# A hybrid decoder layer on one core: small loads moved to lanes and other queues, unread products and ordered low parts at two seams

## The chip, the cores and the metric

One core of a Trainium2 chip runs the kernel. The metric is the time of the core in microseconds; the figure for a kernel is the median of its runs. All times here are in us unless marked ns.

## The reference

The reference is one decoder layer on a row block `x` of 256 tokens by 2048 channels, in fp32. Three sub-layers follow one another, each of the form x = x + rmsnorm(f(rmsnorm(x) * gain)) * gain:

```
mixer:  one projection w_in, whose columns go to three head groups
        A  dilated window attention, with a bias looked up in rel_bias_table
        B  causal gating by 128x128 triangular matrices
        C  RWKV-7 time mixing, with decays sigmoid(tanh(h w_lo) w_up + w0)
        then the output projection w_out
cross:  attention of 4 heads over 256 memory tokens (their norm has the gain mem_src_gain)
FFN:    w_up, a causal depthwise convolution of width 3 (taps ffn_conv_w, ffn_conv_b), gelu gate, w_down
```

## The kernel before

**Products.** Weights and activations are fp32. Each 512 KB block of weights is loaded raw (`raw`, four buffers, SP's queue), and `split()` makes two halves from it: ScalarE casts it to a high part `hi` (line 234), VectorE subtracts this from the raw block for the low part `lo` (line 236). TensorE then makes three products for each pair of blocks, high by high, activation low by weight high and activation high by weight low, on lines 266, 268 and 271 in the mixer's projection, 287 in the FFN's first projection and 324, 326 and 330 in the projections that put weights on the moving side. The activation halves `h` come from a transposition of `x` on TensorE (line 389), ScalarE for the high part times the norm's gain (line 375) and VectorE for the low part (line 376). The gains for that are rows in `grow`, turned to columns `gpar` by one transposition on line 469.

**Stages.** The mixer's projection runs to about 300 us, w_out and the cross attention to about 605 us, and the FFN from there to the end. The seam between the last two is the chain of line 1328 (squares of the cross attention's output), line 1340 (the residual sum, `row`), line 389 (transposition), lines 375 and 376 (`h`), line 287 (first FFN product).

**Order.** Each engine takes its instructions in a fixed order that a scheduler writes from priorities, from pins (`issue_after`) and from lanes. A lane is a Python generator whose `yield` gives the planner an amount of TensorE time; the planner lets the projections' products run and puts a lane's next step behind them. The lanes of the mixer are one chain of `decays`, three `keys` and `inverse`, one of `values`, and three `state`.

**What stands in the first 100 us.** The start loads `x` (8 blocks) and the first weight block on SP's queue, `grow` on ScalarE's queue in two parts, and later on SP's queue, between weight blocks, the rows of the small parameters (`prow`), the bias table with its one-hot matrix (`tab`, `oneh`, `lnc`) and the convolution's taps (`crow`). The bias table's product stands on line 531, the taps' transpositions on line 543. `decays` multiplies the tanh block `zl` by three blocks `wa` (line 642), which share one buffer and are loaded on ScalarE's queue (lines 633 and 634), takes sigmoids (line 647) and then exponentials (lines 662 and 663). ScalarE loads a table whenever it changes between the two. GpSimd fills `BN`, `BR` and `ze` (lines 557, 558 and 591) and loads `lg` (line 616).

Of the kernel before, what the change touches and what calls it, by code (L numbers as in the profile page):

```python
# [12 lines left out]
F32 = mybir.dt.float32  # L13
# [159 lines left out]
def hybrid_block(tc, a, out, dbg=None):  # L173
    nc = tc.nc
    dbg = dbg or {}
    with ExitStack() as ctx:
# [50 lines left out]

        def split(rv, nk, nco):
            hi = mk(wp, "hi", 3, (P, 1024), F32R)
# [3 lines left out]
            with tc.high_priority(offset=AHEAD):  # L233
                nc.scalar.copy(hv, rv)  # L234
                with tc.issue_after(gcopy.ins):
                    nc.vector.tensor_tensor(lv, rv, hv.bitcast(F32), op=ALU.subtract)  # L236
# [182 lines left out]

        def over_rows(r):  # L420
# [31 lines left out]
        grow = sp.tile([4 * KT, P], F32, name="grow")  # L452
        with tc.high_priority(offset=4 * AHEAD):
            nc.scalar.dma_start(grow[:3 * KT, :], gains[0:6:2].rearrange("g (k p) -> g k p", p=P))
            nc.scalar.dma_start(grow[3 * KT:, :], a["mem_src_gain"][0].rearrange("(k p) -> k p", p=P))
# [8 lines left out]
        with tc.high_priority(offset=4 * AHEAD):  # L464
            ident = cp.tile([P, P], F32, name="ident")
            make_identity(nc, ident)
            gpar = cp.tile([P, 4 * KT], F32, name="gpar")
            ps = auxp()
            nc.tensor.transpose(ps[:, :4 * KT], grow, ident[:4 * KT, :4 * KT])
            gcopy = nc.vector.tensor_copy(gpar, ps[:, :4 * KT])  # L470
# [30 lines left out]
        for key, src, n in (("mu", a["rwkv_mu"][0], 21), ("w0", a["rwkv_w0"][0], 6),  # L501
# [7 lines left out]
            r0 += n  # L509
        par = cp.tile([P, NPR], F32, name="par")  # L510
        ps = auxp()
        nc.tensor.transpose(ps[:, :NPR], prow[:NPR, :], ident[:NPR, :NPR])
# [10 lines left out]

        tab = sp.tile([REL_BUCKETS, A_HEADS], F32, name="tab")
        nc.sync.dma_start(tab, a["rel_bias_table"])
        oneh = sp.tile([REL_BUCKETS, 384], F32, name="oneh")
        nc.sync.dma_start(oneh, a["c_onehot"])
        lnc = sp.tile([A_HEADS, 384], F32, name="lnc")
        nc.sync.dma_start(lnc, a["c_lncount"])
        ps = auxp()  # L530
        nc.tensor.matmul(ps[:A_HEADS, :384], lhsT=tab, rhs=oneh, start=True, stop=True)
        nc.vector.tensor_tensor(lnc, ps[:A_HEADS, :384], lnc, op=ALU.add)
        toep = dp.tile([A_HEADS, 384], F32, name="toep")
        nc.gpsimd.dma_start(toep, lnc)

        NF = 2 * FT
        cw = cp.tile([P, 4, NF], F32, name="cw")
        crow = sp.tile([P, 4, P], F32, name="crow")
        nc.sync.dma_start(crow[:NF, 0:3, :], a["ffn_conv_w"][0].rearrange("j (n p) -> n j p", p=P))
        nc.sync.dma_start(crow[:NF, 3, :], a["ffn_conv_b"][0].rearrange("(n p) -> n p", p=P))  # L540
        ps = auxp()
        for j in range(4):
            nc.tensor.transpose(ps[:, j * NF:(j + 1) * NF], crow[:NF, j, :], ident[:NF, :NF])
        nc.vector.tensor_copy(cw, ps[:, :4 * NF].rearrange("p (j n) -> p j n", j=4))
# [76 lines left out]
        nc.gpsimd.memset(keep, 1.0)  # L621
# [7 lines left out]
        def decays():  # L629
            sgs, As = [], []  # L630
            for i in range(3):
                wa = mk(rp, "wa", 1, (P, 256))
                nc.scalar.dma_start(wa[0:64, :], a["rwkv_w_up"][0][:, i * 256:(i + 1) * 256])
                nc.scalar.dma_start(wa[64:128, :], a["rwkv_a_up"][0][:, i * 256:(i + 1) * 256])
# [9 lines left out]
                for dst, key, p0, ps in ((sg3, "w0", 0, both[0]), (view(A, c=4, t=P), "a0", 64, both[1])):  # L644
                    for t in range(2):
                        o = dst[:, 2 * t:2 * t + 2, 1:] if p0 == 0 else dst[:, 2 * t:2 * t + 2, :]
                        nc.scalar.activation(o, ps[:, t * S:(t + 1) * S].rearrange("p (c t) -> p c t", c=2),
                                             AF.Sigmoid, bias=pcol(key, 2 * i + t))
# [3 lines left out]
            for i in range(3):  # L652
# [9 lines left out]
                nc.scalar.activation(E2, E, AF.Exp, scale=KAPPA)  # L662
                nc.scalar.activation(E, E, AF.Exp, scale=-KAPPA)
# [787 lines left out]
        def split_sums(x2, add):  # L1451
# [5 lines left out]
            for j in range(KT // 2):  # L1457
# [3 lines left out]
                with tc.issue_after(h3T.last_lo.ins):  # L1461
                    next(split_to)
# [120 lines left out]
```

## Time and profile before

| | |
|---|---|
| median of 3 runs | 1348.78 (1348.06 to 1353.36) |
| profiled execution, its own time | 1352.56 |
| its span | 1350.8 |
| TensorE busy | 1317.6 (98% of the span) |
| VectorE, ScalarE, GpSimd busy | 65%, 52%, 11% |
| mean granted clock of TensorE | 0.992 |

The profiled execution lies 1.76 us around its span, and 3.78 us above the median. Rows of the trace give the start of an instruction in us from the span's start, its duration, engine, line, operation and tiles; in brackets stands the idle time of the engine before it and what ended it. TensorE's clock is a share of 2.4 GHz: 1.00 is that level, 0.50 is 1.2 GHz.

### The profile page before, as it was taken

To read this page: it belongs to the slowest core of one execution; us is meant where nothing else is said; L and a number is where in the kernel's file an instruction comes from. 1 tells how busy PE (TensorE), PEld (TensorE's weight loads), DVE (VectorE), ACT (ScalarE), POOL (GpSimd) and SP (SyncE) were. 2 spreads that over 40 slices of the span, in tenths; PEclk is the share of its full clock that TensorE was granted. 3 is DMA by queue.
4 is the path that set the end of the run, shared out by engine and by line. 5 is a ranking of instruction groups with operands and counts; after the bars stand their busy time and mean duration, and the time that the engine had idled before them with its cause. 6 is when DMAs were issued, how large, how long until landed. Compare 5 with 4: busy or idle time off the path is not lost.

```text
span 1350.8 us, 20948 instructions
## 1 busy us (share of the span) xinstructions
PE 1317.6 (98%) x8184; PEld 1157.1 (86%) x8184; DVE 873.6 (65%) x1300; ACT 708.3 (52%) x1077; POOL 143.9 (11%) x179
## 2 busy tenths in 40 slices
PE   6899999999999999999999999999999999999997
PEld 6789979998987889879888888888888888888886
DVE  5578974466666666566867677776767674445444
ACT  6665363244456655456655555555555553444442
POOL 3010101120014100000111111111111120000000
PEclk9899999999999999999999999999999999999999
DMA  7444553155447755444666666666666666666553
GB/s 226 138 142 142 156 172 111 40 178 165 141 143 271 251 177 187 156 154 129 195 192 189 188 189 191 193 191 188 188 190 191 193 221 193 196 190 196 191 195 133
DMA packets 189841, 238.82 MB, mean 177 GB/s; under 512 B 7920, under 2 KB 144013, under 8 KB 189741
## 3 DMA queue, kind: packets, MB, share of 16 engines
q1 hardware_dynamic: 185514, 225.23, 53.7%
q0 software_dynamic: 3376, 11.29, 2.5%
q8 instruction: 64, 1.05, 0.3%
q10 hardware_dynamic: 851, 0.95, 0.2%
q14 instruction: 36, 0.29, 0.1%
HBM read 235.33 MB, written 2.12 MB: 176 GB/s over the span
## 4 chain that ended last, share of the span: by engine, by line
PE 93%; DVE 2%; issue 1%; DMA 1%; ACT 1%; POOL 1%; ACTq 0%; DVEq 0%; POOLq 0%
PE mm L302 23%; PE mm L304 11%; PE mm L324 11%; PE mm L326 11%; PE mm L330 11%; PE mm L271 6%; PE mm L266 5%; PE mm L268 5%; PE mm L287 2%; DMA wa<-in_rwkv_w_up_dram 1%; PE auxq L678 1%; DVE lo L236 1%; DMA raw<-in_w_in_dram 0%; PE auxp L389 0%; PE auxq L389 0%
## 5 line engine op out<-in xcount | busy, mean ns | idle before, releaser
L236 DVE TENSOR_TENSOR lo<-raw,hi 128x1024 fp32r<-128x1024 f32 x422 | 519.4, 1232 | 368.4 <-ACT hi L234 365.4
L234 ACT CAST hi<-raw 128x1024 fp32r<-128x1024 f32 x422 | 443.4, 1051 | 438.2 <-PE mm L326 169.1
L302 PE MATMUL mm<-h,hi 128*128 128x512 f32 x1344 | 466.2, 394 | 0.0
L304 PE MATMUL mm<-h,lo 128*128 128x256 f32 x1344 | 372.3, 277 | 0.0
L302 PEld LDWEIGHTS mm<-h,hi 128*128 128x128 f32 x1344 | 252.0, 188 | 58.6
L304 PEld LDWEIGHTS mm<-h,lo 128*128 128x128 f32 x1344 | 252.2, 188 | 0.0
L266 PE MATMUL mm<-h,hi 128*128 128x256 f32 x592 | 155.2, 293 | 1.6 <-ACT h L375 1.6
L268 PE MATMUL mm<-h,hi 128*128 128x256 f32 x592 | 152.3, 288 | 0.0
L324 PE MATMUL mm<-hi,hid 128*128 128x512 f32 x352 | 136.9, 389 | 0.0
L326 PE MATMUL mm<-hi,hid 128*128 128x512 f32 x352 | 136.9, 389 | 0.0
L266 PEld LDWEIGHTS mm<-h,hi 128*128 128x128 f32 x592 | 115.6, 196 | 3.9 <-ACT h L375 1.8
L268 PEld LDWEIGHTS mm<-h,hi 128*128 128x128 f32 x592 | 115.4, 195 | 0.4 <-issue 0.3
L1498 POOL TENSOR_TENSOR z<-z,rrow 128x256 f32<-128x256 f32 x84 | 70.2, 836 | 397.3 <-DVE z L1497 397.3
L330 PE MATMUL mm<-lo,hid 128*128 128x512 f32 x352 | 108.3, 389 | 0.0
L271 PE MATMUL mm<-h,lo 128*128 128x256 f32 x592 | 99.1, 289 | 0.0
L271 PEld LDWEIGHTS mm<-h,lo 128*128 128x128 f32 x592 | 84.1, 196 | 1.9 <-issue 1.6
L324 PE MATMUL mm<-hi,h 128*128 128x512 f32 (+1 forms) x208 | 79.2, 386 | 1.7 <-ACT hi L234 1.7
L324 PEld LDWEIGHTS mm<-hi,hid 128*128 128x128 f32 x352 | 66.1, 188 | 13.8
L330 PEld LDWEIGHTS mm<-lo,hid 128*128 128x128 f32 x352 | 66.1, 188 | 13.7
L326 PEld LDWEIGHTS mm<-hi,hid 128*128 128x128 f32 x352 | 66.0, 188 | 13.6
L326 PE MATMUL mm<-hi,h 128*128 128x512 f32 (+1 forms) x208 | 77.0, 375 | 0.0
L330 PE MATMUL mm<-lo,h 128*128 128x512 f32 (+1 forms) x208 | 59.8, 375 | 0.2 <-DVE lo L236 0.2
(352 smaller groups left out, 1547.5 us busy)
## 6 DMA issues: line engine op xcount, KB each, us to landing
raw<-in_ffn_w_up_dram SPq DMA_DIRECT2D x176, 512.0 KB, 4.6
raw<-in_w_in_dram SPq DMA_DIRECT2D x94, 512.0 KB, 4.3
raw<-in_ffn_w_down_dram SPq DMA_DIRECT2D x88, 512.0 KB, 4.9
raw<-in_w_out_dram SPq DMA_DIRECT2D x32, 512.0 KB, 4.6
raw<-in_mem_wkv_dram SPq DMA_DIRECT2D x16, 512.0 KB, 4.0
raw<-in_mem_wq_dram SPq DMA_DIRECT2D x8, 512.0 KB, 3.4
raw<-in_mem_wo_dram SPq DMA_DIRECT2D x8, 512.0 KB, 3.8
x<-in_x_dram SPq DMA_DIRECT2D x8, 256.0 KB, 6.7
```

Of the source, the lines that this page charges most:

```text
L234: nc.scalar.copy(hv, rv)
L236: nc.vector.tensor_tensor(lv, rv, hv.bitcast(F32), op=ALU.subtract)
L266: nc.tensor.matmul(o, lhsT=hv[:, k, cs], rhs=X.h(k0 + k), start=(k0 + k == 0), stop=False)
L268: nc.tensor.matmul(o, lhsT=hv[:, k, cs], rhs=X.l(k0 + k), start=False, stop=False)
L271: L.last = nc.tensor.matmul(o, lhsT=lv[:, k, cs], rhs=X.h(k0 + k), start=False, stop=(k0 + k == nk - 1))
L287: L.last = nc.tensor.matmul(ps[g][t][:, :S], lhsT=w[:, k, cs], rhs=x(k0 + k), start=(k0 + k == 0 and i == 0), stop=(k0 + k == KT - 1 and i ...
L302: nc.tensor.matmul(view(ps[t], z=2, t=S), lhsT=hv[:, k, cs], rhs=X.hl[k0 + k], start=(k0 + k == 0), stop=False)
L304: L.last = nc.tensor.matmul(ps[t][:, S:], lhsT=lv[:, k, cs], rhs=X.h(k0 + k), start=False, stop=(k0 + k == KT - 1))
L324: nc.tensor.matmul(o, lhsT=X.h(kk)[:, ts_], rhs=hv[:, k, :], start=(first and k0 + k == 0), stop=False)
L326: nc.tensor.matmul(o, lhsT=X.l(kk)[:, ts_], rhs=hv[:, k, :], start=False, stop=False)
L330: L.last = nc.tensor.matmul(o, lhsT=X.h(kk)[:, ts_], rhs=lv[:, k, :], start=False, stop=(last and k0 + k == nk - 1))
L1498: nc.gpsimd.tensor_tensor(z, z, got["x2row"], op=ALU.mult)
```

## The change

1. The loads of the bias table and of the taps leave SP's queue and the start of the program. A new lane `tables()` issues them from GpSimd's queue into the buffer `ze`, after GpSimd has set `keep`, and makes the product and the transpositions two steps later.
2. The three `wa` blocks have three buffers and all six loads are issued at once from GpSimd's queue, also after `keep`. The exponentials are pinned behind the last sigmoid, which leaves two table loads in this part where there were six.
3. `grow` holds 48 rows. The gain of the memory's norm goes alone into `grow2`, on SP's queue behind `prow`, and has a transposition of its own.
4. `keep_busy(n)` issues n products of the identity with itself whose result nothing reads: seven ahead of the gains' transposition, ten behind the last product of the cross attention's output projection.
5. At the FFN's seam the low parts `lo` of the first weight blocks are pinned: the second behind the residual sum of the second row block, the third behind the sums of the step j = 1.
6. `keys` yields 5.5 where it yielded 3.5.

```diff
+        lo_pins = []
+
         def split(rv, nk, nco):
+            pin = lo_pins.pop(0) if lo_pins else None
...
                 nc.scalar.copy(hv, rv)
-                with tc.issue_after(gcopy.ins):
+                with tc.issue_after((pin or gcopy).ins):
                     nc.vector.tensor_tensor(lv, rv, hv.bitcast(F32), op=ALU.subtract)
...
+        def keep_busy(n):
+            ps = auxq()
+            for _ in range(n):
+                r = nc.tensor.matmul(ps[:, :P], lhsT=ident, rhs=ident, start=True, stop=True)
+            return r
...
-        grow = sp.tile([4 * KT, P], F32, name="grow")
+        grow = sp.tile([3 * KT, P], F32, name="grow")
+        grow2 = sp.tile([KT, P], F32, name="grow2")
         with tc.high_priority(offset=4 * AHEAD):
-            nc.scalar.dma_start(grow[:3 * KT, :], gains[0:6:2].rearrange("g (k p) -> g k p", p=P))
-            nc.scalar.dma_start(grow[3 * KT:, :], a["mem_src_gain"][0].rearrange("(k p) -> k p", p=P))
+            nc.scalar.dma_start(grow, gains[0:6:2].rearrange("g (k p) -> g k p", p=P))
...
+            r = keep_busy(7)
             ps = auxp()
-            nc.tensor.transpose(ps[:, :4 * KT], grow, ident[:4 * KT, :4 * KT])
-            gcopy = nc.vector.tensor_copy(gpar, ps[:, :4 * KT])
+            with tc.issue_after(r.ins):
+                nc.tensor.transpose(ps[:, :3 * KT], grow, ident[:3 * KT, :3 * KT])
+            gcopy = nc.vector.tensor_copy(gpar[:, :3 * KT], ps[:, :3 * KT])
...
+        nc.sync.dma_start(grow2, a["mem_src_gain"][0].rearrange("(k p) -> k p", p=P))
...
+        nc.tensor.transpose(ps[:, P:P + KT], grow2, ident[:KT, :KT])
+        nc.vector.tensor_copy(gpar[:, 3 * KT:], ps[:, P:P + KT])
...
-        tab = sp.tile([REL_BUCKETS, A_HEADS], F32, name="tab")
-        nc.sync.dma_start(tab, a["rel_bias_table"])
...
-        crow = sp.tile([P, 4, P], F32, name="crow")
-        nc.sync.dma_start(crow[:NF, 0:3, :], a["ffn_conv_w"][0].rearrange("j (n p) -> n j p", p=P))
...
-        nc.gpsimd.memset(keep, 1.0)
+        keep_set = nc.gpsimd.memset(keep, 1.0)
...
         def decays():
             sgs, As = [], []
-            for i in range(3):
-                wa = mk(rp, "wa", 1, (P, 256))
-                nc.scalar.dma_start(wa[0:64, :], a["rwkv_w_up"][0][:, i * 256:(i + 1) * 256])
-                nc.scalar.dma_start(wa[64:128, :], a["rwkv_a_up"][0][:, i * 256:(i + 1) * 256])
+            was = [s1() for _ in range(3)]
+            for i, wa in enumerate(was):
+                with tc.issue_after(keep_set.ins):
+                    nc.gpsimd.dma_start(wa[0:64, :], a["rwkv_w_up"][0][:, i * 256:(i + 1) * 256])
+                    nc.gpsimd.dma_start(wa[64:128, :], a["rwkv_a_up"][0][:, i * 256:(i + 1) * 256])
+            for i, wa in enumerate(was):
...
-                nc.scalar.activation(E2, E, AF.Exp, scale=KAPPA)
-                nc.scalar.activation(E, E, AF.Exp, scale=-KAPPA)
+                with tc.issue_after(sig.ins):
+                    nc.scalar.activation(E2, E, AF.Exp, scale=KAPPA)
+                    nc.scalar.activation(E, E, AF.Exp, scale=-KAPPA)
...
-            yield 3.5
+            yield 5.5
...
+        def tables():
+
+            yield 30.0
+            t = mk(rp, "ze", 1, (P, 3072))
+            rows, lnc, crow = t[:REL_BUCKETS, 0:512], t[:A_HEADS, 512:896], view(t[:, 1024:1536], j=4, c=P)
+            with tc.issue_after(keep_set.ins):
+                nc.gpsimd.dma_start(rows[:, :A_HEADS], a["rel_bias_table"])
+                nc.gpsimd.dma_start(rows[:, P:P + 384], a["c_onehot"])
+                nc.gpsimd.dma_start(lnc, a["c_lncount"])
+                nc.gpsimd.dma_start(crow[:NF, 0:3, :], a["ffn_conv_w"][0].rearrange("j (n p) -> n j p", p=P))
+                nc.gpsimd.dma_start(crow[:NF, 3, :], a["ffn_conv_b"][0].rearrange("(n p) -> n p", p=P))
+            yield 10.0
+            ps = auxp()
+            nc.tensor.matmul(ps[:A_HEADS, :384], lhsT=rows[:, :A_HEADS], rhs=rows[:, P:P + 384], start=True, stop=True)
+            nc.vector.tensor_tensor(lnc, ps[:A_HEADS, :384], lnc, op=ALU.add)
+            nc.gpsimd.dma_start(toep, lnc)
+            yield 1.0
+            ps = auxp()
+            for j in range(4):
+                nc.tensor.transpose(ps[:, j * NF:(j + 1) * NF], crow[:NF, j, :], ident[:NF, :NF])
+            nc.vector.tensor_copy(cw, ps[:, :4 * NF].rearrange("p (j n) -> p j n", j=4))
...
         L.add(chain(decays(), *(keys(i) for i in range(3)), inverse()))
+        L.add(tables())
...
             split_to = transposed(h3T, x2, gcol(2), hbuf, paired=True)
+            with tc.issue_after(L.last.ins):
+                L.last = keep_busy(10)
             add(0, 0)
             h3T.last_lo = add(1, 0)
+            lo_pins.extend([None, h3T.last_lo])
             for j in range(KT // 2):
...
-                with tc.issue_after(h3T.last_lo.ins):
+                with tc.issue_after(h3T.last_lo.ins), tc.issue_after(L.last.ins):
                     next(split_to)
+                if j == 1:
+                    lo_pins.append(h3T.last_lo)
```

The orders below show three places; line numbers after the change are 4 to 28 higher. The first is ScalarE at the program's start, before: `hi_290` and `hi_320` are the high parts of the first and second weight block, `h` the high parts of the activations.

```order
L234 CAST hi_290<-raw_80 128x1024
L408 ACTIVATE tmp_200,rpart_195<-x_82 128x512
L408 ACTIVATE tmp_202,rpart_195<-x_84 128x512
L375 ACTIVATE h_112<-auxp_107,gpar 128x256
L375 ACTIVATE h_123<-auxq_118,gpar 128x256
L375 ACTIVATE h_112<-auxp_107,gpar 128x256
L375 ACTIVATE h_134<-auxp_129,gpar 128x256
L375 ACTIVATE h_123<-auxq_118,gpar 128x256
L375 ACTIVATE h_145<-auxq_140,gpar 128x256
L375 ACTIVATE h_134<-auxp_129,gpar 128x256
L375 ACTIVATE h_156<-auxp_151,gpar 128x256
L234 CAST hi_320<-raw_318 128x1024
```

The same place after the change:

```order
L238 CAST hi_282<-raw_80 128x1024
L412 ACTIVATE tmp_208,rpart_203<-x_82 128x512
L412 ACTIVATE tmp_210,rpart_203<-x_84 128x512
L238 CAST hi_312<-raw_310 128x1024
L379 ACTIVATE h_120<-auxp_115,gpar 128x256
L238 CAST hi_350<-raw_348 128x1024
L379 ACTIVATE h_131<-auxq_126,gpar 128x256
L379 ACTIVATE h_120<-auxp_115,gpar 128x256
L379 ACTIVATE h_142<-auxp_137,gpar 128x256
L379 ACTIVATE h_153<-auxq_148,gpar 128x256
```

The casts of the second and third weight block have moved from behind eight `h` to ahead of the first and second.

The second place is TensorE at the decays, before (`zl` is the tanh block, `wa` the first of the three up-projections; the other two stand 34 and 75 rows further on):

```order
L271 MATMUL mm_543<-h_112,lo_547 128x256 x2
L271 MATMUL mm_543<-h_123,lo_547 128x256
L642 MATMUL auxp_380<-zl,wa_374 128x256
L642 MATMUL auxp_381<-zl,wa_374 128x256
L642 MATMUL auxp_380<-zl,wa_374 128x256
L642 MATMUL auxp_381<-zl,wa_374 128x256
L271 MATMUL mm_543<-h_123,lo_547 128x256
L266 MATMUL mm_543<-h_134,hi_585 128x256
```

The same place after the change, from the end of the first up-projection (`s_65`) to the end of the third (`s_67`):

```order
L641 MATMUL auxp_379<-zl,s_65_366 128x256
L272 MATMUL mm_347<-h_187,hi_488 128x256
L270 MATMUL mm_347<-h_197,hi_488 128x256
L272 MATMUL mm_347<-h_198,hi_488 128x256
L270 MATMUL mm_347<-h_197,hi_488 128x256
L272 MATMUL mm_347<-h_198,hi_488 128x256
L641 MATMUL auxp_421<-zl,s_66_367 128x256 x2
L275 MATMUL mm_347<-h_186,lo_489 128x256 x2
L275 MATMUL mm_347<-h_197,lo_489 128x256 x2
L270 MATMUL mm_534<-h_120,hi_538 128x256
L272 MATMUL mm_534<-h_121,hi_538 128x256
L641 MATMUL auxp_422<-zl,s_66_367 128x256 x2
```

The three up-projections now stand close together, with about a dozen products of the projection between the first and the last.

The third place is VectorE at the FFN's seam, before (each L1340 ends the residual sum of one row block, L357 and L1330 begin that of the second, L376 is the first low activation):

```order
L1340 SCALAR_TENSOR_TENSOR row_6158<-row_6158,small_6310,yg_4751 128x512
L236 TENSOR_TENSOR lo_6431<-raw_6428,hi_6430 128x1024
L236 TENSOR_TENSOR lo_6488<-raw_6485,hi_6487 128x1024
L357 SCALAR_TENSOR_TENSOR small_6312<-part_6117,fs_6259 128x1
L1330 TENSOR_TENSOR row_6306<-mm_6263,gb_5856 128x512
L1340 SCALAR_TENSOR_TENSOR row_6162<-row_6162,small_6314,yg_4755 128x512
L376 SCALAR_TENSOR_TENSOR h_6323<-auxp_6318,gpar,h_6323 128x256
```

The same place after the change:

```order
L1363 SCALAR_TENSOR_TENSOR row_6166<-row_6166,small_6318,yg_4759 128x512
L361 SCALAR_TENSOR_TENSOR small_6320<-part_6125,fs_6267 128x1
L1353 TENSOR_TENSOR row_6314<-mm_6271,gb_5864 128x512
L1363 SCALAR_TENSOR_TENSOR row_6170<-row_6170,small_6322,yg_4763 128x512
L240 TENSOR_TENSOR lo_6450<-raw_6447,hi_6449 128x1024
L380 SCALAR_TENSOR_TENSOR h_6342<-auxp_6337,gpar,h_6342 128x256
```

Two low parts no longer stand between the residual sums of the two row blocks; one comes behind both, the other later.

## Rows read from the trace of the kernel before

**Rows 1.** The page: busy time of each engine, share of the span, instructions.
```profile
PE 1317.6 (98%) x8184; PEld 1157.1 (86%) x8184; DVE 873.6 (65%) x1300; ACT 708.3 (52%) x1077; POOL 143.9 (11%) x179
```

**Rows 2.** TensorE's waits: who waited, for what, total, times, longest.
```profile
PE auxp L469 <- DMA grow<-in_mem_src_gain_dram: 7.9, 1, 7.9
PE auxp L389 <- DVE row L1340: 3.2, 2, 2.9
...
PE auxp L713 <- ACT et L703: 1.6, 1, 1.6
PE mm L266 <- ACT h L375: 1.6, 1, 1.6
PE auxp L642 <- DMA wa<-in_rwkv_w_up_dram: 1.3, 1, 1.3
```

**Rows 3.** Stretches: length, busy time by engine, granted clock, DMA share, GB/s.
```profile
19.50:22.70 3.20, 3.20 (x18) 3.20 (x16) 3.07 (x5) 3.20 (x9) 0.00 (x0) 0.50 0.77 240
37.00:43.30 6.30, 6.30 (x26) 5.08 (x25) 1.58 (x2) 1.04 (x1) 0.55 (x1) 0.50 0.41 116
57.00:60.50 3.50, 3.50 (x19) 3.50 (x18) 2.84 (x3) 2.93 (x5) 0.00 (x0) 0.51 0.63 183
610.00:613.40 3.40, 3.40 (x18) 3.40 (x18) 2.61 (x5) 1.06 (x3) 0.00 (x0) 0.50 0.08 27
```

**Rows 4.** Timeline of the start: start, duration, engine, line, operation, tiles, wait.
```profile
2.19 6.87 SPq L437 DMA_DIRECT2D x<-in_x_dram  x6
...
10.18 0.46 ACT L375 ACTIVATE h<-auxp,gpar 128x256 fp32r<-128x256 f32 x1
...
11.48 0.56 PE L266 MATMUL mm<-h,hi 128*128 128x256 f32 x1
...
13.38 0.60 PE L389 MATMUL auxq<-ident,x 128*128 128x128 f32 x4
...
15.59 1.04 ACT L234 CAST hi<-raw 128x1024 fp32r<-128x1024 f32 x1 [2.00 <-DMA raw<-in_w_in_dram]
...
23.39 0.50 ACT L375 ACTIVATE h<-auxq,gpar 128x256 fp32r<-128x256 f32 x1
```

**Rows 5.** Timeline of TensorE at the bias table's product.
```profile
36.86 1.43 PE L531 MATMUL auxp<-oneh,tab 32*12 32x384 f32 x2 [2.22 <-issue]
```

**Rows 6.** Timeline of VectorE ahead of it.
```profile
30.70 2.90 DVE L515 TENSOR_SCALAR omu<-par 128x21 f32<-128x21 f32 x1
...
34.32 1.23 DVE L236 TENSOR_TENSOR lo<-raw,hi 128x1024 fp32r<-128x1024 f32 x1 [0.70 <-DMA raw<-in_w_in_dram]
```

**Rows 7.** Timeline of GpSimd at the same time.
```profile
29.89 0.75 POOL L616 DMA_DIRECT2D lg<-in_rwkv_ln_gain_dram  x1
...
30.88 2.69 POOL L591 MEMSET ze<- 128x3072 f32 x1
```

**Rows 8.** The page's DMA issues: KB each, median us to landing.
```profile
raw<-in_w_in_dram SPq DMA_DIRECT2D x94, 512.0 KB, 4.3
...
lg<-in_rwkv_ln_gain_dram POOLq DMA_DIRECT2D x1, 384.0 KB, 5.7
wa<-in_rwkv_ln_bias_dram POOLq DMA_DIRECT2D x3, 128.0 KB, 3.3
```

**Rows 9.** Timeline of ScalarE: two of the first set's sigmoids.
```profile
51.60 0.84 ACT L647 ACTIVATE ca<-auxp,par 128x256 f32<-128x256 f32 x2
```

**Rows 10.** Timeline of VectorE at the FFN's seam.
```profile
605.41 1.22 DVE L236 TENSOR_TENSOR lo<-raw,hi 128x1024 fp32r<-128x1024 f32 x1 [0.20 <-issue]
606.56 0.15 DVE L357 SCALAR_TENSOR_TENSOR small<-part,fs 128x1 f32<-128x1 f32 x1
...
610.65 1.41 DVE L1340 SCALAR_TENSOR_TENSOR row<-row,small,yg 128x512 f32<-128x512 f32 x2
```

**Rows 11.** Timeline of ScalarE there: end of the squares' sum.
```profile
605.85 0.19 ACT L1328 ACTIVATION_READ_ACCUMULATOR tmp<-mm 128x1 f32 x1
```

**Rows 12.** A stretch of the mixer with its lanes, columns as in rows 3.
```profile
160.00:180.00 20.00, 20.00 (x159) 19.02 (x158) 19.41 (x38) 8.32 (x10) 1.91 (x2) 1.00 0.49 146
```

More of the change, by code (lines that the diff above doesn't have):

```diff
@@ L521, in pcol @@
             return par[:, off[key] + i:off[key] + i + 1]
-        tab = sp.tile([REL_BUCKETS, A_HEADS], F32, name="tab")
-        nc.sync.dma_start(tab, a["rel_bias_table"])
[L526 to L534, printed above, removed]
         NF = 2 * FT
         cw = cp.tile([P, 4, NF], F32, name="cw")
-        crow = sp.tile([P, 4, P], F32, name="crow")
-        nc.sync.dma_start(crow[:NF, 0:3, :], a["ffn_conv_w"][0].rearrange("j (n p) -> n j p", p=P))
[L540 to L544, printed above, removed]
+        toep = dp.tile([A_HEADS, 384], F32, name="toep")
         start.close()
@@ L646, in decays @@
                         o = dst[:, 2 * t:2 * t + 2, 1:] if p0 == 0 else dst[:, 2 * t:2 * t + 2, :]
-                        nc.scalar.activation(o, ps[:, t * S:(t + 1) * S].rearrange("p (c t) -> p c t", c=2),
-                                             AF.Sigmoid, bias=pcol(key, 2 * i + t))
+                        sig = nc.scalar.activation(o, ps[:, t * S:(t + 1) * S].rearrange("p (c t) -> p c t", c=2),
+                                                   AF.Sigmoid, bias=pcol(key, 2 * i + t))
                 sgs.append(sg)
```

## The prediction, made before the changed kernel ran

> **What bounds the kernel now.** I read the busy times first: TensorE works for 98% of the span [rows 1], so the change can only win where TensorE waits or runs slowly, and lose where it makes TensorE wait. The list of TensorE's waits came next; the reader is to see that the largest lie in two places, the first 80 us and the seam ahead of the FFN [rows 2]. The stretches show the second kind of loss: in four of them the granted clock is 0.50 or 0.51, the 1.2 GHz level, each behind a wait of TensorE [rows 3]. A stretch at half clock loses about half its length: 1.6 us from 19.5, 3.15 from 37, 1.7 from 57 and 1.7 from 610. So what is to be had is some 18 us of waits and 8 us of clock, of which the 7.9 us at the very start mostly wait for x and the first weights as well. The timelines of single engines then show what ends each wait.
>
> What a measurement of this kernel can tell from no change is 0.5%, 6.7 us. The working below is in the profiled execution's terms (1352.56 us); the median of the runs is 3.78 us lower, and I take the same difference off both.
>
> **The start: the gains' load, unread products, order of ScalarE.** The gains' transposition waited 7.9 us for the second part of `grow` [rows 2], and that goes. Seven unread products take its place; four records of a 128x128 transposition last 0.60 us [rows 4], so fourteen records last about 2.1, in a gap of 7.9: they cost nothing, and if the cover were gone, 2.1. What is late next is in ScalarE's order: the casts of the second and third weight block now stand ahead of the first and second `h`. Before, the first `h` ran at 10.18 and the second block's cast at 15.59, after 2.00 us of waiting for the block [rows 4]. SP's issues of x lasted 6.87 us [rows 4]; without the `grow` load's part in them I estimate the block 3 us sooner at best, so its cast begins between 12.6 and 15.6 and the first `h` between 13.6 and 16.6. Everything behind that cast on ScalarE waits with it: the other `h`, and with them TensorE's first real products, at 11.48 before [rows 4], now near 15. Walking ScalarE's new order with the old durations, the last `h` of x ends at 29.5 in place of 23.9 (23.39 and 0.50, [rows 4]), 5.6 later. TensorE gets back its 1.6 us wait for `h` [rows 2] and about half of the 1.6 us of clock, since it then runs without breaks: 5.6 - 1.6 - 0.8 = **3.2 lost**. Bounds: none lost, if the products catch up before they next wait for weights, and 5.6 lost.
>
> **The tables.** Their product waited 2.22 us for its turn [rows 5], and 6.3 us at half clock followed [rows 3], 2.2 + 3.15 = 5.4 together. With the product gone from there, the next limit is the weights: VectorE's low part at 34.32 waited 0.70 us for a raw block [rows 6], so TensorE would have found its next block late in any case. I count two thirds, **3.6 gained**; the bounds are 0.7 and 5.4. The product itself, 1.43 us at half clock [rows 5], is made later at full clock: **0.7 gained**. SP's queue loses five small loads there, which only helps the raw blocks. On GpSimd's queue these five stand ahead of the first power of the `keys`; at 0.75 us an issue [rows 7] that is under 4 us, some 30 us of planned work before it is wanted: nothing. `grow2` goes on SP's queue behind the small parameters and its transposition beside theirs; its column is first read in the cross attention, so it costs nothing either.
>
> **The decays.** Before, TensorE waited 1.3 us for a `wa` [rows 2] and lost 1.7 us of clock after it: 3.0, gone. Two new waits stand against it. The six `wa` loads now queue on GpSimd's queue behind `lg`, issued at 29.89 and landing in 5.7, and a 128 KB load of that queue takes 3.3 by itself [rows 7, 8]. So the first `wa` lands near 40, when TensorE comes to it; a wait between nothing and 5.7 us, of which I take 1.8. Second, the three sets stand close together with about a dozen products between the first and the last, and two PSUM buffers serve all three: a set waits until four sigmoids have emptied the buffers before it. Two sigmoids last 0.84 us [rows 9], four 1.7, twice 3.4, a weight cast of 1.04 [rows 4] stands between them, and the dozen products hide some 1.4: 3.4 + 1.0 - 1.4 = 3.0. Sum: 3.0 - 1.8 - 3.0 = **1.8 lost**, between 3.0 gained and 7.3 lost (1.6 of clock lost again would be at this end too). Four table loads go from ScalarE, which so comes sooner to the keys' `et`; TensorE's wait of 1.6 us for that on line 713 [rows 2] I count as **1.6 gained**, with nothing as the lower bound.
>
> The Trainium skill has a rule that speaks against this part. The page "SBUF — State Buffer", section "SBUF: two separate sides", says that GpSimd writes the descriptors of the loads it issues, through a port pair that it shares with VectorE, and that such a load stalls while VectorE runs an operation that holds the pair; a load from ScalarE's or SP's queue does not. The rows show the pair at work the other way round: a 21-column operation of VectorE lasted 2.90 us and ended with GpSimd's fill of `ze` [rows 6, 7]. For the loads they show little: 384 KB from GpSimd's queue landed in 5.7 and 128 KB in 3.3, against 4.3 for 512 KB from SP's [rows 8]. By the rule `wa` would land later than I take it, by the rows not.
>
> **The `ze` fill.** It moves from 30.88 to behind the tables' use of that buffer. There VectorE is fuller, and the fill can hold one small operation for up to 2.7 us [rows 7]; TensorE sees that only if VectorE has no slack. I take nothing, with 2.7 lost as the other end.
>
> **The seam.** The transposition of the second residual sum waited 2.9 us [rows 2]. ScalarE had the sum of squares at 606.04 (605.85 and 0.19, [rows 11]), but VectorE took it up only at 606.56, behind a low part that began at 605.41 and lasted 1.22 [rows 10]. With both low parts out of the way, and the last output product 0.3 us earlier because no transposition stands ahead of it, the chain from there to the transposition comes 0.5 + 0.3 = 0.8 sooner. Ten unread products are twenty records, by the row above at most 3.0 us and by their pitch nearer 2.1, in a gap of 2.9: hidden. If the clock stays at the upper level, the 1.7 us of the stretch from 610 come back too [rows 3]. But TensorE, then twice as fast, meets VectorE's residual sums, a pair of 1.41 us [rows 10], and I take 0.6 off. 0.8 + 1.7 - 0.6 = **1.9 gained**, between 0.2 (the clock falls anyway) and 2.5.
>
> **The rest.** From 80 us to the end of the mixer the lanes' order changes by permutation (`keys` yields two units more, three times), and the FFN's order behind the seam is the same. The mixer's VectorE is the one to watch: 19.41 of 20 us from 160, with TensorE full [rows 12]. I take nothing here, with 3 either way.
>
> **Sum.** -3.2 + 3.6 + 0.7 - 1.8 + 1.6 + 1.9 = 2.8 gained. 1352.56 - 2.8 = 1349.8 in the profiled execution's terms, and 1348.78 - 2.8 = **1346.0** for the median.
>
> **Rivals.** First, all covers hold: the start is not held by the cast (3.2 back), the sets' waits for sigmoids are hidden (1.8 back) and the seam gives 2.5 (0.6 more). 1346.0 - 5.6 = 1340.4. For it speaks the wide gap at the start; against it the order of ScalarE, which is fixed. Second, nothing is left over: the clock falls at the seam all the same (1.7 less) and the start loses 5.6 (2.4 more), 1346.0 + 4.1 = 1350.1, the time before within what can be told. For it speaks that each gain stands beside a loss of like size. Third, slower: the `keys` and `inverse` lanes start some 6 us later against the weights, since, by the walk above, the start is that much later, and VectorE has no room to catch up: in the stretch from 160 only 0.6 of 20 us are free [rows 12]. Once the lag exceeds the slack that VectorE has behind the decays, TensorE waits for the lanes at the end of the mixer's projection for what is left: up to 6 us, 1346.0 + 6 = 1352.0, and with the decays at their worst end (5.5 more) 1357.5. Against it: TensorE showed no such wait over 1.6 us in the list before [rows 2]. Fourth, by the page's rule: if the `wa` loads starve, the first set waits 5.7 in place of 1.8, and the clock falls once more (1.7): 1346.0 + 5.6 = 1351.6. The trace bears it out for fills, not for loads.
>
> **How the numbers follow.** The forecast has 0.45 (1342.5 to 1349), the first rival 0.25, the second 0.16, the third 0.10, the fourth 0.04. Faster by over 0.5% means below 1342.0: the first rival for the most part, 0.21, and a little of the forecast, 0.03: 0.24. Slower by over 0.5% means above 1355.5: the third with the decays at their worst end, and a little of the second and fourth, 0.07. The rest, 0.69, is within 0.5%. The range from 1339.0 to 1352.5 holds the forecast, the first two rivals nearly whole and half the third.
>
> **What would show it.** Right at the start: the first `h` behind the second weight cast, near 14 to 16, and TensorE's first real product right after. At the tables: no wait and no half clock from 37 to 43. At the decays: new waits of the up-projections on sigmoids and on `wa`, two table loads in place of six. At the seam: the transposition of the second sum at 0.8 us less behind the last product, and a granted clock of 1.00 from 610. The prediction is wrong if the first real product comes before 12, if the clock at the seam falls again, or if TensorE waits over 3 us for a lane between 100 and 300 us.

## The result, and the profile after

The changed kernel takes 1356.06 us (median of 5 runs, 1355.22 to 1357.2) against 1348.78 before: 1.0047 times as long, with a 95% interval of 1.0031 to 1.0063. (This ratio, like those below, is an estimate from the single runs and need not be the quotient of the medians.) It is slower; the forecast was 1346.0, with a range that ended at 1352.5. The profiled execution took 1356.2, its span is 1354.4, 3.6 more than the span before. Measured by the start of the same weight cast in both traces, the changed kernel is 4.7 us late at 30 us, 10.7 at 48, 3.2 at 118, 5.8 from 341 on, and 3.4 behind the FFN's seam.

TensorE's waits after (as in [rows 2]; line numbers are those of the changed file):

```profile
PE mm L270 <- ACT h L379: 4.4, 1, 4.4
PE mm L334 <- DVE lo L240: 2.9, 1, 2.9
PE auxp L641 <- DMA s<-in_rwkv_w_up_dram: 2.7, 1, 2.7
...
PE auxp L641 <- ACT oc L646: 0.8, 1, 0.8
...
PE auxp L641 <- ACT ca L646: 0.4, 1, 0.4
```

The waits for `grow`, for the bias table and for `et` are gone, as forecast; so is the long one at the seam. New are the wait at the start for the first activation, the one at the output projection for a low part, and those at the decays for the load of the first up-projection and for sigmoids.

Stretches after (columns as in [rows 3]):

```profile
37.00:42.00 5.00, 2.28 (x20) 2.10 (x19) 2.34 (x4) 1.38 (x2) 2.96 (x10) 1.00 0.99 258
42.40:59.50 17.10, 15.89 (x59) 11.86 (x56) 8.07 (x12) 11.21 (x21) 2.33 (x5) 0.50 0.38 96
192.50:196.00 3.50, 3.50 (x9) 2.73 (x10) 3.36 (x4) 2.16 (x3) 0.00 (x0) 0.51 0.62 185
610.00:613.40 3.40, 3.13 (x28) 2.86 (x27) 1.78 (x4) 1.47 (x3) 0.54 (x1) 1.00 0.00 0
```

The half clock of [rows 3] at 37 and at 610 is gone. In its place one stretch of 17.1 us at 0.50 follows the 2.7 us wait for the decays' load; at half clock it loses up to 8.5 us. A second fall, behind the wait of 2.9 near 190, loses another 1.7.

ScalarE and TensorE at the start (as in [rows 4]):

```profile
14.72 1.04 ACT L238 CAST hi<-raw 128x1024 fp32r<-128x1024 f32 x1 [3.61 <-DMA raw<-in_w_in_dram]
15.67 0.47 ACT L379 ACTIVATE h<-auxp,gpar 128x256 fp32r<-128x256 f32 x1
...
28.88 0.47 ACT L379 ACTIVATE h<-auxq,gpar 128x256 fp32r<-128x256 f32 x1
```
```profile
16.19 0.58 PE L270 MATMUL mm<-h,hi 128*128 128x256 f32 x1 [4.45 <-ACT h L379]
```

ScalarE stood idle for 3.61 us in front of a weight cast whose block had not landed, with the activations queued behind it. The first is 5.5 us later than before, and so is the last.

The lateness goes on to GpSimd, which waits for the row factors (ScalarE's squares of x) before its fills, and has the decays' loads behind these:

```profile
28.50 0.71 POOL L421 TENSOR_TENSOR rs<-small,mhalf 128x2 f32<-128x2 f32 x1 [26.36 <-DVE small L420]
29.18 2.65 POOL L554 MEMSET BN<- 128x3072 f32 x1
...
34.39 0.75 POOL L613 DMA_DIRECT2D lg<-in_rwkv_ln_gain_dram  x1
...
35.60 0.57 POOL L631 DMA_DIRECT2D s<-in_rwkv_w_up_dram  x1
```
```profile
41.78 1.88 PE L641 MATMUL auxp<-zl,s 64*128 64x256 f32 x8 [2.72 <-DMA s<-in_rwkv_w_up_dram]
```

`lg` is issued at 34.39, where it was 29.89 before [rows 7]; the loads begin at 35.60, and TensorE, which no longer stops at the bias table, is there before they land.

The seam (as in [rows 10, 11]), ScalarE and TensorE:

```profile
609.83 1.05 ACT L238 CAST hi<-raw 128x1024 fp32r<-128x1024 f32 x1 [0.33 <-PE mm L330]
610.78 0.59 ACT L1351 ACTIVATE tmp<-mm 128x512 f32<-128x512 f32 x1
```
```profile
609.63 0.62 PE L334 MATMUL mm<-lo,oc 128*128 128x512 f32 x2
610.09 2.39 PE L428 MATMUL auxq<-ident 128*128 128x128 f32 x20
...
613.19 0.44 PE L393 MATMUL auxp<-ident,row 128*128 128x128 f32 x2 [0.27 <-DVE row L1363]
```

TensorE at the same place before:

```profile
604.22 0.41 PE L389 MATMUL auxp<-ident,row 128*128 128x128 f32 x2 [0.27 <-DVE row L1340]
...
604.61 0.71 PE L330 MATMUL mm<-lo,oc 128*128 128x512 f32 x2
...
608.24 0.44 PE L389 MATMUL auxp<-ident,row 128*128 128x128 f32 x2 [2.92 <-DVE row L1340]
```

From the end of the last output product (610.25) to the second transposition are 2.9 us, as before: the square now waits for a weight cast on ScalarE. The unread products fill 2.4 of them, and the clock stays up. The last output product itself comes sooner, since the transpositions of the first row block now stand behind it: it begins at 609.63, 5.0 later than before, where the casts ahead of it are 5.8 late.

### The profile page after: what moved, and what is told of

The parts are those of the page before. It is cut to its first block, busy times and chain, and to the rows that moved or that the text cites. A ratio compares the mean times of both kernels' runs of the same rounds, so it can differ in the third digit from the quotient of the medians.

```text
span 1354.4 us, 21026 instructions
## 1 busy us (share of the span) xinstructions
PE 1326.2 (98%) x8219; PEld 1164.1 (86%) x8219; DVE 873.0 (64%) x1301; ACT 703.3 (52%) x1073; POOL 152.5 (11%) x190
## 4 chain that ended last, share of the span: by engine, by line
PE 87%; DVE 5%; issue 5%; POOL 1%; ACT 1%; DMA 0%; DVEq 0%; POOLq 0%; ACTq 0%
PE mm L306 23%; PE mm L308 11%; PE mm L328 11%; PE mm L334 11%; PE mm L330 11%; PE mm L275 4%; PE mm L270 4%; PE mm L272 4%; PE mm L291 2%; DVE lo L240 2%; DVE k L762 1%; DVE et L760 1%; PE auxp L641 1%; PE auxq L678 1%; DMA s<-in_rwkv_w_up_dram 0%
## 5 line engine op out<-in xcount | busy, mean ns | idle before, releaser
L334 PEld LDWEIGHTS mm<-lo,hid 128*128 128x128 f32 x352 | 66.1, 188 | 13.7
L330 PEld LDWEIGHTS mm<-hi,hid 128*128 128x128 f32 x352 | 66.1, 188 | 13.7
```

What stands on the lines that cost most here:

```text
L330: nc.tensor.matmul(o, lhsT=X.l(kk)[:, ts_], rhs=hv[:, k, :], start=False, stop=False)
L334: L.last = nc.tensor.matmul(o, lhsT=X.h(kk)[:, ts_], rhs=lv[:, k, :], start=False, stop=(last and k0 + k == nk - 1))
```

## The experiments

The theories after the trace of the changed kernel: A, the decays cost most, by the wait for their load, the packed sets and the clock; B, the late start costs most. C, D and E come up on the way, and F and G split A. The diffs show the deciding lines. Each kernel was timed beside the kernel before, which gave medians of 1349.3 to 1349.6 in these series.

**The seam alone** on the kernel before:

```diff
+            with tc.issue_after(L.last.ins):
+                L.last = keep_busy(10)
...
+            lo_pins.extend([None, h3T.last_lo])
```

> The kernel before with only the seam's part of the change: ten unread products behind the cross attention's last product and the two ordered low parts. Theory A (the seam won 2.5 us in the changed kernel, 1.7 of it the clock that no longer falls, and everything lost was lost ahead of it): the granted clock is 1.00 through the FFN's start, and the time is 2 to 3 us under that of the kernel before, near 1346. Rival (the seam's gain is only that one profiled execution of before had a fall of the clock that others have not): no difference, 1348 to 1350.

Measured: 1346.23, 0.9969 (0.9955 to 0.9983). Theory A's number. The trace tells a second thing. All that stands ahead of the seam is the kernel before, with the same wait at the bias table (2.33 us, 2.22 before), but:

```profile
37.54 0.80 PE L540 MATMUL auxp<-oneh,tab 32*12 32x384 f32 x2 [2.33 <-issue]
```
```profile
37.00:43.30 6.30, 5.76 (x45) 5.15 (x46) 2.21 (x3) 1.05 (x1) 0.91 (x2) 1.00 0.55 157
57.00:60.50 3.50, 3.50 (x31) 3.47 (x29) 3.35 (x5) 3.47 (x6) 0.00 (x0) 1.00 0.68 187
604.00:607.50 3.50, 3.15 (x27) 2.90 (x25) 2.96 (x5) 1.31 (x3) 0.00 (x0) 1.00 0.36 112
```

Two of the falls of [rows 3], at 37 and at 57, did not come in this execution, so the kernel before does not have them each time. How usual they are, the mean granted clock tells, which is known for every execution: in the 86 of the kernel before in these series it lies between 0.992 and 0.997, 0.995 in the median. The profiled one had 0.992. The 14 executions at 0.997 have a median of 1347.6 us, the 6 at 0.992 one of 1353.1.

**The decays as before**, all else changed:

```diff
-            was = [s1() for _ in range(3)]
...
+                wa = mk(rp, "wa", 1, (P, 256))
+                nc.scalar.dma_start(wa[0:64, :], a["rwkv_w_up"][0][:, i * 256:(i + 1) * 256])
...
-                with tc.issue_after(sig.ins):
```

> The changed kernel with the decays as before: one wa buffer, loads on ScalarE's queue, exponentials not pinned, so the three sets stand apart again. Theory A (the decays cost most: a wait of 2.7 us for wa, then sets that wait for sigmoids, and 17 us at half clock): the stretch at 0.50 after 42 us is gone or at most 7 us long, and 6 to 9 of the changed kernel's 1356.1 come back, 1347 to 1350. Theory B (the start costs most: the first activations wait 4.5 us for a weight cast and nothing later makes it good): at most 3 come back, 1353 to 1356.

Measured: 1348.98, 0.9994 (0.9983 to 1.0004); 7.1 come back, and the half clock at the decays shrinks to 3.4 us, as theory A said; but the start is as late as in the changed kernel (first real product at 16.8).

**Without the seven unread products**, all else changed:

```diff
-            r = keep_busy(7)
             ps = auxp()
-            with tc.issue_after(r.ins):
-                nc.tensor.transpose(ps[:, :3 * KT], grow, ident[:3 * KT, :3 * KT])
+            nc.tensor.transpose(ps[:, :3 * KT], grow, ident[:3 * KT, :3 * KT])
```

> The changed kernel without the seven unread products at the first load, and nothing else changed. ScalarE's order has then the first eight activations ahead of the second weight cast, as before. Theory A (the decays cost most): the start is 4 us earlier, but TensorE then comes earlier to the wa loads and waits for them longer, and the half clock stays: 1 to 3 come back, 1353 to 1355. Theory B (the start costs most): 4 to 6 come back, 1350 to 1352, with the first products at 11 to 12 us.

Measured: 1347.86, 0.9985 (0.9974 to 0.9996): 8.2 come back, more than either theory gave. The decays' loads are issued at 30.56 in place of 35.60 and TensorE waits 1.6 us for one and 1.3 for sigmoids there. The first real product, the first load and the clock at the decays:

```profile
11.11 0.58 PE L270 MATMUL mm<-h,hi 128*128 128x256 f32 x1
```
```profile
30.56 0.55 POOL L629 DMA_DIRECT2D s<-in_rwkv_w_up_dram  x1
```
```profile
42.00:49.00 7.00, 7.00 (x28) 6.07 (x29) 5.63 (x9) 5.22 (x9) 0.00 (x0) 0.51 0.01 4
```

The stretch at half clock is about 7 us long, not 17. So the parts do not add up singly: the late start is paid a second time at the decays.

**The first `wa` loaded at the start:**

```diff
-            was = [s1() for _ in range(3)]
+            was = [mk(rp, "wa", 1, (P, 256)), s1(), s1()]
...
+                eng = nc.gpsimd if i else nc.scalar
```

> The changed kernel with the first of the three wa blocks in a buffer of its own and loaded at the start on ScalarE's queue; the other two as in the change. Theory A1 (the wait of 2.7 us for wa is what brings the clock down): no wait for wa, no long stretch at 0.50, 5 to 9 come back, 1347 to 1351. Theory A2 (the sets' pace, each waiting for sigmoids, holds the clock down by itself): the clock is at 0.50 for 10 us or more all the same, and 1 to 4 come back, 1352 to 1355.

Measured: 1351.81, 1.0012 (1.0 to 1.0024). Inconclusive between A1 and A2: the wait only moved to the second load (2.6), and the half clock lasted 13.7.

**The seven unread products alone** on the kernel before:

```diff
+            r = keep_busy(7)
             ps = auxp()
+            with tc.issue_after(r.ins):
+                nc.tensor.transpose(ps[:, :4 * KT], grow, ident[:4 * KT, :4 * KT])
```

> The kernel before with only the seven unread products ahead of the gains' transposition. ScalarE's order then has the second and third weight cast ahead of the first and second activation, as in the change. Theory C (these casts hold the start 4 to 5 us, whatever stands later): first real product at 15 to 17, 1352 to 1355. Theory D (the late start costs only together with the new decays, by the clock there; alone it is absorbed by the waits at the bias table): 1348 to 1350.

Measured: 1354.47, 1.0031 (1.0018 to 1.0044), the first real product at 17.5, behind this wait:

```profile
PE mm L266 <- ACT h L375: 6.4, 1, 6.4
```

Theory C; D falls. The mean clock, 0.995 in the median of the nine executions, is that of the kernel before, so the 4.8 us are not lost to the clock.

**The casts pinned** behind the activations, the unread products kept:

```diff
+                hpin = hi_pins.pop(0) if hi_pins else None
+                with tc.issue_after(hpin.ins) if hpin else ExitStack():
+                    nc.scalar.copy(hv, rv)
...
+        hi_pins.extend([None, hT.his[7], hT.his[9]])
```

> The changed kernel with its seven unread products, and the casts of the second and third weight block pinned behind the eighth and tenth high activation, so that ScalarE's order at the start is nearly that of before. Theory C (the order on ScalarE is the cause, not the unread products' time): first real product at 10 to 12.5, the wait of 4.4 for an activation gone, 1346 to 1350. Rival (the unread products themselves delay the transpositions of x): the first product after 13, 1353 to 1356.

Measured: 1342.48, 0.9953 (0.9936 to 0.9969), less than theory C gave; the first real product:

```profile
10.33 0.58 PE L273 MATMUL mm<-h,hi 128*128 128x256 f32 x1
```

So it is the order on ScalarE, not the time of the unread products.

**The keys' yield as before**, without the seven:

```diff
-            yield 5.5
+            yield 3.5
```

> The changed kernel without the seven unread products and with the keys' yield at 3.5 as before. Theory E (the two more units, three times, push the inverse's steps 6 units later, so that VectorE is still in them when the output projection wants its low parts): the wait of 2.9 near 190 is gone, and the time is 2 to 4 under the kernel without the unread products (1347.9), 1344 to 1346. Rival (the later decays or the tables' hold of ze push the inverse): the wait stays, 1347 to 1349.

Measured: 1346.88, 0.9977 (0.9964 to 0.9991). The wait of 2.9 for a low part is gone, as E said. But a wait for weight casts at the same projection, which the kernel before had too, is back; the first line is of before, the second of this run:

```profile
PE mm L324 <- ACT hi L234: 1.7, 2, 1.1
```
```profile
PE mm L328 <- ACT hi L238: 1.7, 2, 1.1
```

2.9 less 1.7 leaves 1.2; the time is 1.0 lower, less than E gave and within both intervals.

**The decays as before**, without the seven (the edits of the second and third experiment together):

```diff
-            r = keep_busy(7)
...
-            was = [s1() for _ in range(3)]
...
+                wa = mk(rp, "wa", 1, (P, 256))
```

> The changed kernel without the seven unread products and with the decays as before. Theory A (packed decays keep the clock down also from a good start: 6.8 us at 0.50 and 2.9 of waits in the kernel without the unread products): the stretch at half clock shrinks to 3.4 or none, 1344 to 1346.5. Rival (that kernel's clock fall comes from the wait for weights there, whatever the decays do): no difference, 1347 to 1349.

Measured: 1341.87, 0.9944 (0.9928 to 0.996): 6.0 less than with the packed decays, and lower than theory A gave. The mean clock is 0.997 in the median, against 0.993 with them. The clock at the decays:

```profile
36.00:60.00 24.00, 22.37 (x180) 21.33 (x179) 16.39 (x23) 22.77 (x35) 0.56 (x1) 1.00 0.56 156
```

**All three `wa` loaded in the first 12 us**, with the late start:

```diff
-            was = [s1() for _ in range(3)]
+            was = [mk(rp, "wa", 1, (P, 256)), nat()[:, :256], nat()[:, :256]]
...
+                nc.scalar.dma_start(wa[0:64, :], a["rwkv_w_up"][0][:, i * 256:(i + 1) * 256])
```

> The changed kernel, late start and unread products included, with the three wa blocks in buffers that are free from the beginning and loaded by ScalarE's queue in the first 12 us; the packed order of the decays is kept. Theory A1 (TensorE's wait of 2.7 us for the late wa loads is what brought the clock down for 17 us): no wait for a wa, the stretch at 0.50 after 40 us gone or 3.4, 1346 to 1350. Theory A2 (the packed sets, each waiting for the sigmoids before it, bring the clock down by themselves): 6.8 us or more at 0.50 all the same, 1351 to 1355.

Measured: 1352.3, 1.0022 (1.0011 to 1.0032). No wait for a `wa`, and 6.8 us at half clock there instead of 17.1: A2 by the number. The loads had also delayed the start to 18.2, so it is not clean.

**What is left**, without the seven, decays and yield as before (the edits above together):

```diff
-            r = keep_busy(7)
...
+                wa = mk(rp, "wa", 1, (P, 256))
...
+            yield 3.5
```

> The changed kernel without the seven unread products, with the decays and the keys' yield as before: what is left of the change is the split of the gains' load, the tables' lane and the seam. Theory E (the two more units of the keys cause the wait of 2.9 near 190 and the clock after it): 2 to 3 under the kernel with the longer yield (1341.9), 1338 to 1340, no wait for a low part at the output projection's start. Rival (the wait only moves): 1341 to 1343.

Measured: 1341.01, 0.9938 (0.992 to 0.9956), the best of all. Its trace has no fall of the clock until the very end. The step from 1341.87 is within the intervals and in the rival's range, not in E's; the wait of 1.7 for weight casts is back here too.

**The casts pinned, the keys' yield as before:**

```diff
+        hi_pins.extend([None, hT.his[7], hT.his[9]])
...
+            yield 3.5
```

> The changed kernel with the casts pinned behind the activations (1342.5) and the keys' yield as before. Theory E: the wait of 2.9 and the 3.4 us at half clock after it are gone, 1338.5 to 1341. Rival (the gain is eaten by waits of the lanes elsewhere, as with 1 us only in the kernel without the unread products): 1341 to 1343.

Measured: 1346.5, 0.9975 (0.9963 to 0.9987), 4 more where 2 less were expected. Up to the decays this program and the one with the longer yield have the same order on every engine. The decays in the two traces, first with the longer yield, then with the shorter, and how long the up-projections' loads took to land:

```profile
38.00:52.00 14.00, 12.73 (x89) 11.47 (x90) 9.25 (x15) 13.26 (x24) 1.73 (x4) 1.00 0.40 110
```
```profile
DMA to landing us min/median/max: 3.4/4.0/4.4
```
```profile
38.30:52.00 13.70, 12.12 (x43) 9.36 (x44) 7.10 (x11) 7.90 (x16) 3.27 (x6) 0.50 0.40 106
```
```profile
DMA to landing us min/median/max: 5.0/5.4/6.1
```

Issued 0.9 us later and landing 1.4 us later still, the loads made TensorE wait 2.9 us, and 13.7 us at half clock followed, with half as many products.

**The casts pinned, decays and yield as before:**

```diff
+        hi_pins.extend([None, hT.his[7], hT.his[9]])
...
+                wa = mk(rp, "wa", 1, (P, 256))
...
+            yield 3.5
```

> The changed kernel with the casts pinned, and the decays and the keys' yield as before: the candidate with all three repairs. Each repair's own place shows: first real product at 10 to 11, no stretch at half clock at the decays, no wait of 2.9 near 190. If the repairs add up, 1337 to 1340; if the packed decays were a gain once their loads are in time, this is slower than the one with the new decays, 1340 to 1343.

Measured: 1346.49, 0.998 (0.9965 to 0.9995). The repairs do not add up: in this order the decays come at another place among the products, and TensorE waits 2.1 for `et` and 1.4 and 0.6 for `wa`. The packed decays in the same order with the same yield took as long (1346.5), so here they cost nothing. Why it lies 5.5 above the one without unread products is not settled.

**Early loads, packed sets, good start** (the edit of the early loads, without the seven):

```diff
-            r = keep_busy(7)
...
+            was = [mk(rp, "wa", 1, (P, 256)), nat()[:, :256], nat()[:, :256]]
```

> The changed kernel without the seven unread products and with the three wa blocks loaded by ScalarE's queue in the first 12 us; the decays stay packed. Beside it stand the same with the loads on GpSimd's queue (1347.9) and the same with the decays as before (1341.9). Theory F (the late loads are what the decays cost): no wait for wa, clock at 1.00 from 36 to 60, 1341 to 1343. Theory G (the packing, sets that wait for sigmoids, costs it by the clock): a stretch at 0.50 of 6.8 or more, 1345 to 1348.

Measured: 1347.02, 0.9983 (0.997 to 0.9996). Theory G. TensorE at the decays:

```profile
34.93 1.13 PE L638 MATMUL auxp<-zl,wa 64*128 64x256 f32 x8
38.90 1.86 PE L638 MATMUL auxp<-zl,nat 64*128 64x256 f32 x8 [1.94 <-ACT oc L643]
41.02 2.80 PE L638 MATMUL auxp<-zl,nat 64*128 64x256 f32 x8
```

No set waits for its load, the second waits 1.94 for sigmoids, the third then runs at half clock, which lasts 6.8 us. So the packed sets, with their pinned exponentials, cost most of the 6 also with early loads: 5.2, of which up to 1.0 is a later start (first real product at 12.05, 11.02 with the decays as before).

**The pinned casts once more,** no edit beside that of the first time:

> The kernel with the pinned casts once more (1342.5), to see how much of its 4 us to the same kernel with the shorter keys' yield (1346.5) is the chance of when the wa loads land, since the two programs are alike up to the decays and one waited 2.9 for them and one did not. If it is the landing, this gives 1344 to 1347 with some runs near 1342; if it is the yield, 1342 to 1343 again.

Measured: 1344.74, 0.9959 (0.9941 to 0.9977), single runs from 1341.59 to 1347.76, in the range given for the landing. So part of the difference of 4 is chance. Whether the rest is the yield's is not shown: the eleven runs with the longer yield have a median of 1343.2, the ten with the shorter 1346.5, and the one execution traced here had its loads land early (3.8 in the median) and kept the clock at 1.00 there.

## Why the prediction was wrong

Two terms of the sum failed. The decays, put at 1.8 lost less 1.6 gained at `et`, cost 6.0: the wait for `wa` was taken at 1.8, and the clock behind it at nothing but for the far end of the bounds. The start, put at 3.2 lost, cost 8.2: its lateness was counted once, and not again at the decays.

| part | forecast | measured | from |
|---|---|---|---|
| seven unread products, late start | 3.2 lost | 8.2 lost; 4.8 alone | 1356.1 - 1347.9; 1354.5 - 1349.6 |
| packed decays, with `et` | 0.2 lost | 6.0 lost | 1347.9 - 1341.9 |
| keys' yield ("the rest") | nothing | 0.9 lost, within the intervals | 1341.9 - 1341.0 |
| tables' lane, split of the gains' load | 4.3 gained | 5.2 gained | 1346.2 - 1341.0 |
| seam | 1.9 gained | 3.1 gained | 1349.4 - 1346.2 |

The measured column takes the change back step by step, so it adds up by construction; in another order the shares differ (7.1 for the decays with the seven in place, nothing for them with the casts pinned and the shorter yield). The tables' row had no run of its own: it is what lies between two others.

- **The start.** The forecast saw the new order on ScalarE, and its times held: first `h` between 13.6 and 16.6 (15.67), the last at 29.5 (29.35), TensorE's first product near 15 (16.19). Two things failed. It priced the seven unread products by their 2.1 us in an idle gap, "they cost nothing", and gave the order no cause; they are the cause, through the scheduler. And it took 5.6 us of lateness as 3.2 lost once. GpSimd's fills and loads hang on the same order of ScalarE, and so the start was late for the decays as well: with the seven, 17.1 us at half clock there in the profiled execution; without, about 7. Over all executions the difference is smaller: the mean clock is 0.991 with the seven and 0.993 in the median without, worked out some 24 and some 19 us at half clock. That makes about 2.8 us, beside the 4.8 of the late start alone.
- **The decays.** This is the step whose size was most wrong. The forecast took `lg` ahead of the loads at 29.89, its old time, although its own walk had the start 5.6 later; it came at 34.39. The two waits were forecast at 1.8 and 3.0, and came at 2.7 and 1.2. What followed them was left at the far end of the bounds as "1.6 of clock lost again": it was 17.1 us at half clock, which costs up to 8.5. The clock did not rise until the packed sets, each waiting for ScalarE, were past. The far end of the bounds, 7.3, was near. By the mean clock it was not one execution alone: the changed kernel had 0.991 in four of five and 0.986 in the fifth, where the kernel before never fell below 0.992 in the 86.
- **The tables.** Wait and half clock went, and the sum is near, in part by luck: the 3.15 us of clock in it came from one execution, and the seam's experiment has the wait without the fall.
- **The seam.** Right for the clock (1.7) and for the sum of the chain, 0.8, but not for its parts: the 0.5 from VectorE did not come, since with its low parts out of the way ScalarE's weight cast ahead of the square was next; the last output product, which was to be 0.3 earlier, was 0.8 earlier against the casts. Between the weight casts on either side the traces show 2.5 us gained, which is the two together; the 0.6 taken off for VectorE's residual sums did not show.
- **The rivals.** The third, a lag of the lanes that shows at the end of the mixer's projection, came true in kind (2.9 us for a low part near 190, 1.7 of clock), but its cause is the keys' yield, and the yield as before took it away for no more than 1 us, since the wait for weight casts came back. The fourth, by the rule of the Trainium skill (page "SBUF — State Buffer", section "SBUF: two separate sides"), had the loads late: 64 KB took 5.5 to 6.8 us from GpSimd's queue in the changed kernel. Whether VectorE's operations held them back is not shown; with a good start, loading from ScalarE's queue brought 0.8 us, within the intervals. So the rule did not decide the time.
- **The median.** The forecast took the profiled execution's half-clock stretches for the kernel's. The 3.8 us between it and the median were a sign that they were not all: by its mean clock of 0.995 a usual execution of before spends some 13 us at half clock, the profiled one, at 0.992, some 22.
- **The signs.** None of the three that were to show the prediction wrong appeared (first real product at 16.2, clock at the seam 1.00, no wait over 2.9 us between 100 and 300). None of them lay at the decays.

Left open: why repairs that each work do not add up with the pinned casts, why the packed decays cost nothing there, and what the landing of GpSimd's small loads depends on.

## What to carry to other kernels

An instruction whose own time is hidden can still move others: read the new order on every engine behind it, and price the first thing that then waits for a transfer. A wait of TensorE can cost more than its length (here 2.7 us and up to 8.5 of clock, where small products that waited for ScalarE followed it), so spread small products among dense ones, and give their inputs a margin of several us. And before a stretch at half clock is booked as a gain, see it in more than one execution, or compare the mean clock of many.

## What the runs showed of the hardware

The same order of instructions gave 1341.59 and 1347.76 us in one series. Where two traces of one order up to the decays could be compared, the loads behind the fills took 4.0 and 5.4 us to land (medians), and the clock there was at 1.00 in one and at 0.50 for 13.7 us in the other.

With the packed decays the stretch at half clock was 17.1, 13.7 and 13.7 us where TensorE had waited 2.6 to 2.9 us for a load, and 6.8 (four traces) or none (two) where its longest wait there was 1.3 to 1.9, for ScalarE or for a load. A wait does not settle it: the one of 2.9 us for a low part at the output projection was followed by 3.4 us at half clock in five traces, by 6.8 in two and by none in two.
